# Tile slots, decay order and diagonal-block stores where DeltaNet periods meet mLSTM heads

## The chip, the cores and the metric

The kernel runs on one core of one Trainium2 chip. The metric is the device time of one execution in microseconds (us). The engines are TensorE (PE; its weight loads are a track of their own, PEld), VectorE (DVE), ScalarE (ACT), GpSimd (POOL) and SyncE (SP), which here issues the DMAs. Each engine takes its instructions in the order in which the program issued them.

## The reference

One decoder layer in float32, sequence 256, width 2048:

```
h = RMSNorm_pre(x) * (1 + scale) + shift        [shift | scale | gate] = silu(c) W_ada + b_ada
[gdn_qkv | a | b | gdn_z | ml_qk | ml_v | i | f | ml_o | ml_z | g_A | g_B] = h W_in
y_A = W_pA( RMSNorm_head(GatedDeltaNet(conv(q, k, v), decay, beta)) * silu(gdn_z) )
y_B = W_pB( sigmoid(ml_o) * RMSNorm_head(mLSTM(conv(q, k), v, i, f)) * silu(ml_z) )
out = (sigmoid(g_A) * y_A + sigmoid(g_B) * y_B) W_out
x <- x + gate * RMSNorm_post(out)
```

The DeltaNet branch has 16 query/key heads and 32 value heads of width 128, the mLSTM branch 8 heads with keys of 128 and values of 256. DeltaNet needs a triangular solve for each head; mLSTM needs decayed scores, their product with the values, and a normalisation.

## The kernel before

**A stream of weights.** All matmuls with weights go through one stream. A unit is a tile of 128 x 2048 weights (1 MB), loaded by SP into one of three buffers `raw` (L164). A unit has two pieces of 1024 columns; each is prepared by a cast on ACT (`whi`, L169) and a subtraction on DVE (`wlo`, L170), in four buffers each, up to four pieces ahead of PE. A product is then three matmuls, high by high, high by low and low by high (L223). A unit's load is issued once the unit three before it has been prepared.

**Side work in steps.** Everything else is written as generators. After each piece that PE uses, one side step runs every generator up to its next `yield`, in order of rank: the second half of a DeltaNet period first (rank 0), then scores, convolutions and mLSTM (rank 1), then the triangular solve (rank 2). So one program order, fixed when the kernel is built, says what stands behind what on each engine; `yield from wait(n)` puts work n steps later. A debt of DVE time holds the solve back (`side.room`); other generators wait for free PSUM banks (`banks`).

**The order of the stream.** After a start phase come eight DeltaNet periods. Each has the projection of an even head pair (8 pieces), a gate projection z (8) and the projection of an odd pair (8). Then come four pairs of mLSTM heads, m = 0 to 3: the q/k projection (tiles 24 + m), the v projection (28 + m), and for m = 0 also two gate projections (32 and 36). Then the projections `py` out of both branches and the output projection `pw`.

**A DeltaNet pair.** `gdn_stage1` does the convolution and Silu (L585 to L590), loads two rows of cumulated decays into `gb` (L603), masks them on POOL into `dd` (L610; one buffer), takes the score products on PE (`psa`, `psb`) and exponentiates `dd` on ACT (L618 to L620). DVE multiplies scores and decays into `au` (L677), the first block one step before the second. After the second pair of a period `base_inverse` stores the 32 x 32 diagonal blocks of both pairs' `au` into DRAM, four stores for each pair (`ud`, L697), loads them back spread over the partitions (`ug`, L701, four loads of 128 KB), and solves on DVE (L708 to L725; one buffer `ug`). The inverse goes out and back once more (`xd`, `xcmp`) and `gdn_stage2` carries on 31 steps later, or at once for the last period: small matmuls `mp`, `mx`, `mq`, `mz`, `pa`, `pb`, `pc`, `po` with ACT's copies between them (`pcm`, `y`, `ys`) and DVE's `rr` (L822); at the end the turned heads go through `oT` (two buffers) to `o_dr` (L884).

**An mLSTM pair.** `mlstm_qk` loads its own `gb`, does the convolution, and in the convolution's second and fourth step issues the mask (into the same `dd`) and the exps. When seven periods have passed `po`, it issues the scores `pss`, their product with the decays (`mst`, L931), then `pnum` against the values `vt` (copied out of PSUM by ACT, L993), squares, denominators, and `hn`. DVE multiplies `hn` by the gates (L1004, L1007); `mlstm_out` turns it on PE (`mpt`, L976), scales it on ACT into `hT` (L980), and stores it to `hb_dr`. `hT` uses the buffers of `oT`.

**The gate of the residual.** silu(c) times the last third of W_ada is summed by DVE: 16 more units of 1 MB in the same stream, in the same three buffers, with two DVE operations each (L1062, L1064, `gacc`) and no PE work. `add_gate_unit` is called once a tile and lets a unit in whenever 24 chunks have come up, 16 for each call; the calls are in the projections of m = 1, 2 and 3. At the end `gate_sum` adds the partitions on PE, and ACT copies the four quarters through one buffer `gr` (tag `ys`), each stored by SP before the next copy may write.

Of the kernel before, what the change touches and what calls it, by code (L numbers as in the profile page):

```python
# [7 lines left out]
F32 = mybir.dt.float32  # L8
# [109 lines left out]
def hybrid_layer_kernel(  # L118
# [99 lines left out]
    def pow_(o, i, e):  # L218
        G.tensor_tensor(o, i, e, op=ALU.pow)  # L219
# [402 lines left out]
    def gdn_stage1(p, ps, res):  # L622

        z = p % 2
        qs = bp.tile([P, 4, S], F32, name="qs", tag="qs")
        qh = bp.tile([P, 2, S], F32R, name="qh", tag="qh", bufs=1)
        yield from conv_silu(ps, lambda n, j: late_c["gcv"][:, (p * 4 + n) * 4 + j:(p * 4 + n) * 4 + j + 1], qs, qh,
                             0 if z else 3)
        gb = decay_rows(2 * p)
        dd = decay_mask(gb)  # L630
        b12 = bp.tile([P, 2], F32, name="b12", tag="b12")
        G.tensor_tensor(b12, gb[:, :, P - 1], ngt[:, 0, 2 * p:2 * p + 2], op=ALU.add)
        side.debt += 0.7
        ql = bp.tile([P, 2, S], F32R, name="ql", tag="ql", bufs=1)
        V.tensor_tensor(ql, qs[:, 0:2], qh.bitcast(F32), op=ALU.subtract)
        yield from wait(2)
        yield from banks(3)
        res["t"] = side.t
        psa = gtile("psa", True)
        mm3(psa, qh[:, 1, 0:P], ql[:, 1, 0:P], qh, ql, True, True)  # L640
        psb = gtile("psb", True)
        mm3(psb[:, 0:256], qh[:, 1, P:S], ql[:, 1, P:S], qh[:, :, P:S], ql[:, :, P:S], True, True)
        for m in range(2):
            T.transpose(psb[:, 256 + m * P:256 + (m + 1) * P], qs[:, 0, m * P:(m + 1) * P], ident)
        psv = gtile("psv", True)
        side.debt -= 1.6
        for blk in range(2):
            for h in range(2):
                T.transpose(psv[:, (blk * 2 + h) * P:(blk * 2 + h + 1) * P],
                            qs[:, 2 + h, blk * P:(blk + 1) * P], ident)  # L650
        decay_exp(dd, gb, ngt[:, 0, 2 * p:2 * p + 2], b12, ngt[:, 1, 2 * p:2 * p + 2])
        sse = bp.tile([P, 4], F32, name="sse", tag="sse", bufs=3)
        junk = bp.tile([P, P], F32, name="junk", tag="sq", bufs=1)
        for m in range(2):
            A.activation(junk, psb[:, 256 + m * P:256 + (m + 1) * P], AF.Square, accum_out=sse[:, m:m + 1])
        yield
        if z == 0:
            res["eq"] = bp.tile([P, 2, 2], F32, name="eq", tag="eq", bufs=3)
            res["rr"] = bp.tile([P, 2, 2, S], F32, name="rr", tag="rr")
        rk = bp.tile([P, 2], F32, name="rk", tag="rk")  # L660
        cj = bp.tile([P, 2, 2], F32, name="cj", tag="cj")
        res["au", z] = au = bp.tile([P, 2, 768], F32, name="au", tag="au", bufs=5)

        side.debt += 1.3
        for blk, ps_, n, c0 in ((0, psa, 256, 0), (1, psb, 128, 512)):
            V.scalar_tensor_tensor(au[:, 0, c0:c0 + P], ps_[:, n:n + P], 1.0, ident, op0=ALU.mult, op1=ALU.mult,
                                   accum_out=sse[:, 2 + blk:3 + blk])
        V.tensor_scalar(sse[:, 2:4], sse[:, 2:4], EPS, None, op0=ALU.add)
        V.reciprocal(rk, sse[:, 2:4])
        V.tensor_tensor(cj, tt[:, :, 32 + 2 * p:34 + 2 * p], rk.unsqueeze(2).broadcast_to([P, 2, 2]), op=ALU.mult)  # L670
        V.tensor_scalar(res["eq"][:, z], sse[:, 0:2], EPS, 128.0 * EPS, op0=ALU.add, op1=ALU.mult)

        for blk, ps_, n, c0 in ((0, psa, 256, 0), (1, psb, 128, 512)):
            yield
            side.debt += 1.45 if blk == 0 else 1.0
            for h in range(2):
                V.scalar_tensor_tensor(au[:, h, c0:c0 + 2 * n].rearrange("p (a b) -> p a b", a=2),  # L677
                                       ps_[:, 0:2 * n].rearrange("p (a b) -> p a b", a=2), cj[:, blk, h:h + 1],
                                       dd[:, h, c0 // 2:c0 // 2 + n].unsqueeze(1).broadcast_to([P, 2, n]),
                                       op0=ALU.mult, op1=ALU.mult)  # L680
            gfree(ps_)
            if blk == 0:
                sk = bp.tile([P, 2], F32, name="sk", tag="sk")
                pow_(sk, sse[:, 2:4], phalf[:, 0:2])
        yield
        for blk in range(2):
            A.activation(res["rr"][:, blk, z], psv[:, blk * S:(blk + 1) * S], AF.Copy, scale=sk[:, blk:blk + 1])
        gfree(psv)

    def base_inverse(zg, res, zr):  # L690

        ud = dr.tile([4, 8, 32, 32], F32, name="ud", tag="ud", bufs=2)
        xd = dr.tile([8, 4, 4, 8, 32], F32, name="xd", tag="xd", bufs=2)
        for zi in range(2):
            auv = res["au", zi].rearrange("p h (b c) -> p (h b) c", b=2)
            for q in range(4):
                SP.dma_start(ud[q, 4 * zi:4 * zi + 4].rearrange("m j i -> j m i"),  # L697
                             auv[32 * q:32 * q + 32, :, 256 + 32 * q:288 + 32 * q])
        ug = bp.tile([P, 32, 32], F32, name="ug", tag="ug", bufs=1)
        for q in range(4):  # L700
            SP.dma_start(ug[32 * q:32 * q + 32],  # L701
# [207 lines left out]
    def mlstm_qk(m, ps, r):  # L909
# [2 lines left out]
        av = [tt[:, b, 64 + 2 * m:66 + 2 * m] for b in range(2)]  # L912
        conv = conv_silu(ps, lambda n, j: late_c["mcv"][:, (m * 4 + n) * 4 + j:(m * 4 + n) * 4 + j + 1], qk)
        for i, _ in enumerate(conv):
            if i == 1:
                ee = decay_mask(gb)
            elif i == 3:
                decay_exp(ee, gb, av[0], av[0], av[1])
            yield
        yield  # L920
        while applied[0] < 7:
            yield
# [45 lines left out]
    def mlstm_out(m, r):  # L968
        while "hn" not in r:
            yield  # L970
        hn = r["hn"]
        for h in range(2):
            pt = gtile("mpt")
            for cc in range(2):
                for b in range(2):
                    T.transpose(pt[:, cc * S + b * P:cc * S + (b + 1) * P], hn[h][:, b, cc * P:(cc + 1) * P], ident)  # L976
            hT = bp.tile([P, 2, S], F32, name="hT", tag="oT")
            for cc in range(2):
                ch = (2 * m + h) * 2 + cc
                A.activation(hT[:, cc], pt[:, cc * S:(cc + 1) * S], AF.Copy, scale=late_c["mnw"][:, ch:ch + 1])  # L980
            ch = (2 * m + h) * 2
            SP.dma_start(hb_dr[ch:ch + 2].rearrange("c d t -> d c t"), hT)
            yield

    def mlstm(m):
# [39 lines left out]
        def gated():  # L1025

            sg = bp.tile([P, 2, 512], F32, name="sg", tag="sz", bufs=3)
            SP.dma_start(sg, gate_dr[7 + m])
            yield from wait(2)
            while "hn" not in r:  # L1030
                yield
            yield
            for b in range(2):
                gate(b, sg[:, b], True)
            yield
            yield from mlstm_out(m, r)
        gate_unit = add_gate_unit if m else None
        add_proj_t(24 + m, lambda ps: side.add(mlstm_qk(m, ps, r)), gate_unit)
# [1 line left out]
        if m:  # L1040
            return
        add_proj_n(32 + m, lambda ps: gate_after(ps, AF.Sigmoid))
        add_proj_n(36 + m, lambda ps: gate_after(ps, AF.Silu))

    gate_at = [0, 0]
    gate_half = []
# [1 line left out]
    def add_gate_unit():  # L1048

        gate_at[1] += KC  # L1050
        if gate_at[1] < 24 or gate_at[0] == KC:
            return
        gate_at[1] -= 24
        i = gate_at[0]
        gate_at[0] += 1

        def prep(h, raw):
            side.debt += 2.4
            for q in range(2):
                if i == 0:  # L1060
                    gate_half.append(bp.tile([P, 1024], F32, name=f"gacc{q}", tag="au", bufs=5))
                    V.tensor_scalar(gate_half[q], raw[:, q * 1024:(q + 1) * 1024], sil[:, 0:1], None, op0=ALU.mult)  # L1062
                else:
                    V.scalar_tensor_tensor(gate_half[q], raw[:, q * 1024:(q + 1) * 1024], sil[:, i:i + 1],  # L1064
                                           gate_half[q], op0=ALU.mult, op1=ALU.add)
            if i == KC - 1:
                side.add(gate_sum())
            return ()
        stream.add(w_ada[32 + i], prep, None, 1)

    def gate_sum():
        yield
        for q in range(4):
            gps = gtile("gps")
            T.matmul(gps[0:1, :], ones, gate_half[q // 2][:, (q % 2) * 512:(q % 2 + 1) * 512], start=True, stop=True)
            gr = bp.tile([1, 512], F32, name="gr", tag="ys", bufs=1)
            A.copy(gr, gps[0:1, :])
            yield
            SP.dma_start(gate_row_dr[:, q * 512:(q + 1) * 512], gr)
# [288 lines left out]
```

## Time and profile before

| | |
|---|---|
| median of 3 runs | 1625.53 us (1624.24 to 1626.09) |
| the profiled execution | 1628.82 us |
| its span, first to last instruction | 1627.0 us |
| mean granted TensorE clock | 0.998 |
| DMA | 372.37 MB, mean 229 GB/s |

The span is cut by stage as follows: up to about 330 us the start, 330 to 1000 the DeltaNet periods, 1000 to 1300 the passage into and through the mLSTM heads, 1300 to 1600 the projections out, then the tail. In the rows of the profile, `L170` is line 170 of the kernel, `out<-in` are the program's names of what an instruction writes and reads, and "idle before" tells how long the engine stood still and which instruction or DMA ended that. Matmuls overlap, so a matmul's duration is longer than its spacing to the next.

### The profile page before, as it was taken

The numbers are of one execution on the slowest core, as the hardware profiler recorded it, in microseconds if no ns is written. First come the engines' busy times: TensorE is split into PE (matmuls) and PEld (weight loads), VectorE is DVE, ScalarE is ACT, GpSimd is POOL, SyncE is SP. The second block draws the span as 40 slices with busy tenths as digits, with TensorE's granted clock in tenths as the row PEclk, the third lists the DMA queues.
The fourth block names the chain that finished last, engine by engine and source line by source line (L and its number), as shares of the span: only waits on it lengthen the run. The fifth ranks groups of instructions, "written<-read, shape, count | busy, mean of one in ns | idle before, by whom it ended". The sixth has DMA issues, their size and how long they took to land. (4 is left out here: it accounts for less than half of the span.)

```text
span 1627.0 us, 25444 instructions
## 1 busy us (share of the span) xinstructions
PE 1590.7 (98%) x9844; PEld 1388.0 (85%) x9844; DVE 1148.0 (71%) x1798; ACT 932.5 (57%) x1496; POOL 234.2 (14%) x191
## 2 busy tenths in 40 slices
PE   7999999899999999999999999999999999999998
PEld 4788888689999999999999999789887788888886
DVE  6685555665689787878787878685778556756654
ACT  7754446665656575757575756565565544444442
POOL 1787761000000000000000100000000000100100
PEclk9999999999999999999999999999999999999999
DMA  9898775665465545555555455547788668766573
GB/s 378 334 408 329 267 285 183 242 253 196 163 202 173 186 165 185 179 181 180 180 181 180 168 177 190 160 164 263 266 313 316 223 236 300 275 238 246 200 272 117
DMA packets 96261, 372.37 MB, mean 229 GB/s; under 512 B 26262, under 2 KB 46214, under 8 KB 58252
## 3 DMA queue, kind: packets, MB, share of 16 engines
q1 hardware_dynamic: 96140, 370.75, 64.3%
q8 instruction: 77, 1.26, 0.3%
q14 instruction: 44, 0.36, 0.1%
HBM read 354.40 MB, written 16.31 MB: 228 GB/s over the span
## 5 line engine op out<-in xcount | busy, mean ns | idle before, releaser
L170 DVE TENSOR_TENSOR wlo<-raw,whi 128x1024 fp32r<-128x1024 f32 x454 | 561.0, 1245 | 253.4 <-ACT whi L169 252.3
L169 ACT CAST whi<-raw 128x1024 fp32r<-128x1024 f32 (+1 forms) x517 | 530.3, 1046 | 304.8 <-PE pn L223 136.7
L223 PE MATMUL pt<-h_hi,whi 128*128 128x256 f32 x1280 | 368.8, 288 | 0.0
L223 PE MATMUL pt<-h_hi,wlo 128*128 128x256 f32 x1280 | 363.0, 284 | 0.0
L223 PE MATMUL pt<-h_lo,whi 128*128 128x256 f32 x1280 | 362.8, 283 | 0.0
L223 PE MATMUL pn<-whi,h_hi 128*128 128x512 f32 x896 | 354.3, 395 | 8.2 <-ACT whi L169 6.2
L223 PE MATMUL pn<-wlo,h_hi 128*128 128x512 f32 x896 | 352.3, 393 | 6.1 <-DVE wlo L170 5.2
L223 PE MATMUL pn<-whi,h_lo 128*128 128x512 f32 x896 | 350.2, 391 | 0.0
L223 PEld LDWEIGHTS pt<-h_hi,whi 128*128 128x128 f32 x1280 | 245.9, 192 | 1.4
L223 PEld LDWEIGHTS pt<-h_lo,whi 128*128 128x128 f32 x1280 | 245.9, 192 | 0.3
L223 PEld LDWEIGHTS pt<-h_hi,wlo 128*128 128x128 f32 x1280 | 245.8, 192 | 0.2 <-DVE wlo L170 0.2
L223 PEld LDWEIGHTS pn<-wlo,h_hi 128*128 128x128 f32 x896 | 168.9, 188 | 47.4 <-DVE wlo L170 13.1
L223 PEld LDWEIGHTS pn<-whi,h_hi 128*128 128x128 f32 x896 | 168.9, 188 | 46.6 <-ACT whi L169 7.0
L223 PEld LDWEIGHTS pn<-whi,h_lo 128*128 128x128 f32 x896 | 168.8, 188 | 34.8
L170 POOL TENSOR_TENSOR wlo<-raw,whi 128x1024 fp32r<-128x1024 f32 (+1 forms) x63 | 146.3, 2332 | 67.0 <-ACT whi L169 64.2
L223 PE MATMUL py<-whi,yhi 128*128 128x512 f32 x384 | 150.7, 392 | 1.2 <-ACT vt L993 1.2
L223 PE MATMUL py<-whi,ylo 128*128 128x512 f32 x384 | 149.6, 389 | 0.0
L223 PE MATMUL py<-wlo,yhi 128*128 128x512 f32 x384 | 149.4, 389 | 0.0
L409 DVE TENSOR_TENSOR part<-pn,part 128x512 f32<-128x512 f32 x112 | 73.5, 684 | 52.7 <-PE pn L223 52.7
L169 ACT CAST yhi<-ya 128x512 fp32r<-128x512 f32 x48 | 29.8, 622 | 128.4 <-PE py L223 124.2
L170 DVE TENSOR_TENSOR ylo<-ya,yhi 128x512 fp32r<-128x512 f32 x48 | 33.2, 692 | 90.5 <-ACT yhi L169 88.6
L585 DVE SCALAR_TENSOR_TENSOR qs<-pt,gcv,qs 128x255 f32<-128x255 f32 (+2 forms) x192 | 92.1, 480 | 4.6
(244 smaller groups left out, 1782.2 us busy)
## 6 DMA issues: line engine op xcount, KB each, us to landing
raw<-in_dram SPq DMA_DIRECT2D x259, 1024.0 KB
ar<-in_dram SPq DMA_DIRECT2D x32, 1024.0 KB
raw<-in_dram SPq DMA_DIRECT2D x16, 512.0 KB
ya<-o_dr SPq DMA_DIRECT2D x32, 256.0 KB
gate_dr<-part SPq DMA_DIRECT2D x11, 512.0 KB
gb<-rows SPq DMA_DIRECT2D x20, 256.0 KB
raw<-in_dram SPq DMA_DIRECT2D x6, 768.0 KB
ug<-ud SPq DMA_DIRECT2D x32, 128.0 KB
```

Source lines behind the costliest of these rows:

```text
L169: A.copy(hi, src)
L170: (eng or V).tensor_tensor(lo, src, hi.bitcast(F32), op=ALU.subtract)
L223: T.matmul(ps, l, r, start=start and i == 0, stop=stop and i == 2, skip_group_check=True)
L409: V.tensor_tensor(part[g][:, b], ps[b], part[g][:, b], op=ALU.add)
L585: V.scalar_tensor_tensor(dst[:, n, sh:], src[:, 0:S - sh], taps(n, 3 - sh), dst[:, n, sh:], op0=ALU.mult, op1=ALU.add)
```

## The change

- The stores of the diagonal blocks (`ud`) move out of `base_inverse` into `block_rows`, called for each pair in the step of its last score product.
- A counter `scored` tells which pair that was. `mlstm_qk` goes on past the convolution only when it is 15; for m = 0 the mask is then issued one step later and the exps two steps later, no longer within the convolution. For m = 1 to 3 they stay in the convolution.
- `hT` takes the buffers `qh` and `ql` in turn.
- After the gates of m = 1 to 3, `mlstm_out` starts two steps later where it was one.
- Gate units are let in also during the second gate projection of m = 0 (4 more calls, 28 in all), one for every 28 chunks; there are still 16, and the last comes with the same call.
- The two sums `gacc` take a buffer of `ug` and one of `rr` where they had two of the five of `au`; the four quarters `gr` take buffers of `on` (two), `p2` and `tmp`.

```diff
@@ gdn_stage1
             if blk == 0:
                 sk = bp.tile([P, 2], F32, name="sk", tag="sk")
                 pow_(sk, sse[:, 2:4], phalf[:, 0:2])
+            else:
+                scored[0] = p
+        block_rows(res, z)
         yield
...
+    scored = [-1]
+
+    def block_rows(res, z):
+
+        if z == 0:
+            res["ud"] = dr.tile([4, 8, 32, 32], F32, name="ud", tag="ud", bufs=2)
+        auv = res["au", z].rearrange("p h (b c) -> p (h b) c", b=2)
+        for q in range(4):
+            SP.dma_start(res["ud"][q, 4 * z:4 * z + 4].rearrange("m j i -> j m i"),
+                         auv[32 * q:32 * q + 32, :, 256 + 32 * q:288 + 32 * q])
+
     def base_inverse(zg, res, zr):
-        ud = dr.tile([4, 8, 32, 32], F32, name="ud", tag="ud", bufs=2)
+        ud = res["ud"]
         xd = dr.tile([8, 4, 4, 8, 32], F32, name="xd", tag="xd", bufs=2)
-        for zi in range(2):
-            auv = res["au", zi].rearrange("p h (b c) -> p (h b) c", b=2)
-            for q in range(4):
-                SP.dma_start(ud[q, 4 * zi:4 * zi + 4].rearrange("m j i -> j m i"),
-                             auv[32 * q:32 * q + 32, :, 256 + 32 * q:288 + 32 * q])
@@ mlstm_qk
         for i, _ in enumerate(conv):
-            if i == 1:
+            if i == 1 and m:
                 ee = decay_mask(gb)
-            elif i == 3:
+            elif i == 3 and m:
                 decay_exp(ee, gb, av[0], av[0], av[1])
             yield
+        while scored[0] < 2 * 7 + 1:
+            yield
+        if m == 0:
+            yield
+            ee = decay_mask(gb)
+            yield
+            decay_exp(ee, gb, av[0], av[0], av[1])
         yield
@@ mlstm_out
-            hT = bp.tile([P, 2, S], F32, name="hT", tag="oT")
+            hT = bp.tile([P, 2, S], F32, name="hT", tag=("qh", "ql")[h], bufs=1)
@@ mlstm, gated
-            yield
+            yield from wait(2)
             yield from mlstm_out(m, r)
...
-        add_proj_n(36 + m, lambda ps: gate_after(ps, AF.Silu))
+        add_proj_n(36 + m, lambda ps: gate_after(ps, AF.Silu), add_gate_unit)
@@ add_gate_unit
-        if gate_at[1] < 24 or gate_at[0] == KC:
+        if gate_at[1] < 28 or gate_at[0] == KC:
             return
-        gate_at[1] -= 24
+        gate_at[1] -= 28
...
-                    gate_half.append(bp.tile([P, 1024], F32, name=f"gacc{q}", tag="au", bufs=5))
+                    gate_half.append(bp.tile([P, 1024], F32, name=f"gacc{q}", tag=("ug", "rr")[q], bufs=1 + q))
@@ gate_sum
-            gr = bp.tile([1, 512], F32, name="gr", tag="ys", bufs=1)
+            gr = bp.tile([1, 512], F32, name="gr", tag=("on", "on", "p2", "tmp")[q], bufs=(2, 2, 1, 1)[q])
```

## The prediction

> **What bounds the kernel now.** I read the page first, then the busy time of the engines by stage, then TensorE's (PE's) waits in the one stage that has any, then the rows behind each.
>
> ```profile
> span 1627.0 us, 25444 instructions
> ```
>
> ```profile
> 330.00:1000.00 670.00, 669.18 (x5261) 625.93 (x5261) 531.11 (x1032) 423.28 (x732) 37.91 (x68) 1.00 0.55 184
> 1000.00:1300.00 300.00, 289.77 (x1808) 247.88 (x1807) 211.44 (x324) 173.11 (x326) 18.35 (x22) 0.99 0.69 241
> 1300.00:1600.00 300.00, 299.38 (x1337) 247.68 (x1336) 182.51 (x185) 139.52 (x170) 14.57 (x8) 1.00 0.70 251
> ```
>
> Each row has the stretch, its length, then busy us and instructions of PE, PE's weight loads, DVE, ACT and POOL, the granted clock, the DMA share and GB/s. PE is the bound. In the DeltaNet periods (330 to 1000 us) it idles 0.8 us of 670; only 1000 to 1300, where the periods give way to the mLSTM heads, is open: 10.2 us idle, and a clock a little under full. The start lies outside the change. From the last row, with nothing but 512-column products, one takes 300 / 1336 = 0.22 us, a piece of twelve 2.7. So the ceiling is near 12 us, 0.7%. The waits of that stage (total us, times, longest):
>
> ```profile
> PE pn L223 <- DVE wlo L170: 2.7, 3, 1.1
> PE pnum L947 <- issue: 1.3, 1, 1.3
> PE mq L790 <- ACT y L780: 1.3, 1, 1.3
> PE pn L223 <- ACT whi L169: 1.2, 1, 1.2
> PE py L223 <- ACT vt L993: 1.2, 1, 1.2
> PE mpt L976 <- DVE hn L1004: 1.0, 2, 0.6
> PE pc L829 <- DVE rr L822: 0.9, 1, 0.9
> PE psa L223 <- DVE ql L635: 0.5, 1, 0.5
> ```
>
> Eleven stops, 10.1 us: the whole idle time. The question is which the change reaches. I count the side steps from step 0, in which pair 15's scores go to PE; its last score product is issued in step 3.
>
> **Part 1: decays of head pair 0 behind the last scores.** Rows of the timeline, here and below: start, busy us, engine, line, operation, tiles; in brackets the idle time before and what ended it.
>
> ```profile
> 1021.28 0.77 POOL L610 TENSOR_SCALAR_AFFINE_SELECT dd<-gb 128x256 f32<-128x256 f32 x2 [14.45 <-DVE au L677]
> 1021.72 0.40 ACT L618 ACTIVATE dd<-dd,tt 128x128 f32<-128x128 f32 x1 [8.34 <-POOL dd L610]
> ...
> 1023.49 1.03 ACT L169 CAST whi<-raw 128x1024 fp32r<-128x1024 f32 x1
> 1022.96 0.39 PE L223 MATMUL pn<-whi,h_lo 128*128 128x512 f32 x1
> 1024.57 0.50 PE L223 MATMUL pn<-whi,h_hi 128*128 128x512 f32 x1 [1.23 <-ACT whi L169]
> 1025.83 0.50 PE L223 MATMUL pn<-wlo,h_hi 128*128 128x512 f32 x1 [0.76 <-DVE wlo L170]
> ```
>
> The head's mask takes the only dd buffer, so POOL waits for the last reader of pair 15's (L677); ACT, in order, sits on the exps 8.34 us with the weight casts (whi) behind them, until PE runs dry: 1.2 us, and a wlo wait of 0.8 us next. Now the mask is issued in step 7 and the exps in step 8, when dd has long been free. Both stops go. From 1022.96 to 1024.57 is 1.61 us, of which 1.23 idle and 0.22 the usual spacing: a stop costs some 0.15 beyond its idle time.
>
> What is added: Silu of this head (step 5) now precedes the exps, so one more table load.
>
> ```profile
> 1005.00 1.28 ACT L618 ACT_TABLE_LOAD   x1
> 1006.30 0.40 ACT L618 ACTIVATE dd<-dd,ngt 128x128 f32<-128x128 f32 x1
> ...
> 1032.46 1.06 ACT L993 COPY vt<-pn 128x512 f32<-128x512 f32 x2
> 1033.54 0.76 ACT L768 COPY pcm<-mp 32x256 f32<-32x256 f32 x2
> ...
> 1035.61 0.38 ACT L780 ACTIVATE y<-mx 32x256 f32<-32x256 f32 x1 [0.24 <-PE mx L778]
> ```
>
> Load 1.28 and exps 1.77 (1021.72 to 1023.49) make 3.1 us of ACT in step 8, behind which stand one whi and y, which mq reads in step 10. From the end of step 8's matmuls ACT needs about 2.0 (vt, pcm), 3.1, 1.0 and 0.4: y at 6.5; PE gets to mq after two pieces of 2.7 and two groups of small matmuls, at about 6.5. I take 0.1, between nothing and the whole 3.1. The scores that read the exps are issued only in step 17, so nothing else waits.
>
> By the Trainium skill, "ScalarE: Activation LUTs", section "What ACT_TABLE_LOAD costs", a switch also drains for some 1.38 us, 2.66 in all, which would hold mq 1.3 longer and give 1616.3 instead of 1615.0. The trace disagrees: the first exp starts 1.30 us after the load does.
>
> **Part 2: diagonal blocks out pair by pair.**
>
> ```profile
> 1020.29 8.40 SPq L164 DMA_DIRECT2D raw<-in_dram  x2
> 1028.75 0.94 SPq L884 DMA_DIRECT2D o_dr<-oT  x2
> 1029.73 6.04 SPq L697 DMA_DIRECT2D ud<-au  x8
> 1036.37 2.76 SPq L701 DMA_DIRECT2D ug<-ud  x4
> 1039.18 0.92 SPq L164 DMA_DIRECT2D raw<-in_dram  x2
> 1046.49 0.17 DVE L708 TENSOR_SCALAR nsu<-ug 128x15 f32<-128x15 f32 x1 [7.39 <-DMA ug<-ud]
> 1050.00:1075.00 25.00, 22.12 (x116) 18.02 (x115) 24.06 (x46) 14.10 (x30) 0.00 (x0) 1.00 0.40 136
> ```
>
> The eight ud stores and four ug loads stand together in SP's queue and hold it about 9 us: ug lands at 1046.5, after DVE has idled 7.39 us, and the next raw loads are issued only at 1039.18. DVE then runs 24.06 of 25 us to catch up, and PE meets it late three times: twice on wlo (the 2.7 us above less part 1's 0.8, so 1.9) and once on rr (0.9). Now pair 14's four stores left 24 steps before, and pair 15's four follow its last score product: SP takes them at about 1021, between the raw load at 1020.29 and the next, which waits for a later wlo anyway. Before the loads of ug only o_dr remains; without part 1's stall ug is issued near 1028 and, at the old 7 to 10 us from issue to use, is there at 1035 to 1038, when DVE gets there (PE is 2.3 us earlier, so about 1037). Raw loads follow 4 to 9 us sooner. I count all three stops as gone, with nothing gone as the other end. What is queued behind a store's wait is SP's next raw load; in the 330 to 1000 stage the same twelve DMAs stood ahead of raw loads in every period and PE idled 0.8 us, so I cost the earlier places there at nothing.
>
> **Part 3: own place for hT.**
>
> ```profile
> 1103.59 0.84 ACT L980 ACTIVATE hT<-mpt,mnw 128x256 f32<-128x256 f32 x2 [5.55 <-DMA o_dr<-oT]
> 1107.10:1110.50 3.40, 3.40 (x18) 3.40 (x18) 2.14 (x2) 1.82 (x3) 0.00 (x0) 0.51 0.86 315
> ```
>
> hT shares two buffers with oT, whose stores must land first: ACT idles 5.55 us, y comes late, mq waits 1.3. In qh and ql, last read in step 0, it waits for nothing. Right after that stop the granted clock is 0.51 for 3.4 us, 3.4 x 0.49 = 1.7 us lost; I take it as a result of the stop and the small matmuls around it, so it goes too.
>
> **Part 4: the gate's units, sums and row; one more step for mpt.**
>
> ```profile
> 1146.68 2.47 DVE L1064 SCALAR_TENSOR_TENSOR gacc<-raw,sil,gacc 128x1024 f32<-128x1024 f32 x2
> 1155.44 1.04 ACT L169 CAST whi<-raw 128x1024 fp32r<-128x1024 f32 x1 [6.82 <-DMA raw<-in_dram]
> ...
> 1270.83 0.58 ACT L1077 COPY gr<-gps 1x512 f32<-1x512 f32 x1 [5.14 <-DMA gate_row_dr<-gr]
> 1093.99 1.43 DVE L1007 TENSOR_TENSOR hn<-hn,sg 128x256 f32<-128x256 f32 x4
> 1096.94 0.66 PE L976 MATMUL mpt<-con,hn 128*128 128x128 f32 x4
> ```
>
> Raw has three buffers. At 1155 the load that ACT awaits reuses a gate unit's, so it could be issued only after that unit's 2.47 us on DVE ended at 1149.15; vt stands behind that cast, pnum behind vt: the stop called "issue". With 16 units over 28 places the second tile of head pair 2's projection (t26) reuses the last v tile's buffer instead, one to three pieces sooner; I count 1.3 as gone (other end: none). The old pattern now stands at head pair 2's end, where no DeltaNet work is beside it: I take 0.0, at most 1.5.
>
> gr with a place for each quarter drops the wait of 5.14 us in ACT ahead of head pair 3's squares; its hn is gated that much sooner, and mpt comes a step later: both stops (1.0) go. The later step delays only stores into hb_dr that are read long after.
>
> Two units now start beside the last gate projection. The first comes after the triangle solve in DVE's queue; the second puts 2.47 us ahead of L1007. That ended at 1095.4, so now about 1097.9, past mpt's 1096.94; mpt needs three quarters of it first. I take a new stop of 0.8 (0 to 2.5).
>
> **Sum.** Gone: 2.7 + 1.3 + 1.3 + 1.2 + 1.0 + 0.9 = 8.4 of idle time, nine stops x 0.15 = 1.35, the clock's 1.7: 11.4. Stay: py (1.2; nothing of the change stands ahead of that vt copy in ACT's queue) and psa. New: 0.9. Net 10.5. The profiled execution took 1628.8 around its span of 1627.0, so 1618.3; the median shown, 1625.5, is 3.3 lower, and gives 1615.0.
>
> **Rivals.**
> - *DVE's load, not ug, makes it late* (24.06 of 25 speaks for it; 330 to 1000, with the same solve and no stops, against): 1.9 + 0.9 idle and three fills of 0.15 stay, 3.3 more: 1618.3, and to 1622 if pnum's stop and a larger mpt stop stay too.
> - *The clock dip isn't the stop's.* The idle time before it is only 1.3 us. If it comes by itself it stays: 1.7 more, 1616.7. The Trainium skill, "TensorE: Matmul & The Clock Gate", section "Why this matters for your kernels", sides with this: it asks only for no idle gap over some 3 us. By that rule 1616.7; the dip's own row and the absence of another in 1000 to 1300 don't settle it.
> - *The waits move.* The edits work, but raw loads or DVE stop PE elsewhere for as much: 1622.3 to 1628.8, no change.
> - *Slower: SP.* Pair by pair, the even pairs' four stores now sit in SP's queue behind their last score product, ahead of weight loads, in all eight periods. Four take 3.0 us (6.04 / 2). If raw had no slack that is up to 8 x 3.0 = 24: 1639. Above 1.3 a period (10.5 / 8) it ends slower than before. Against it: PE's 0.8 us idle in 330 to 1000 under a 9 us hold of the same queue.
>
> **Chances.** Forecast 0.55 (1612.7 to 1618), DVE's load 0.17, clock 0.09, waits move 0.12, SP 0.07. A measurement of this kernel can tell about 0.2% (3.3 us) from no change; faster by more: 0.55 + 0.17 + 0.09 = 0.81. The range holds these three: low end with py's stop gone too and no new ones (11.4 + 1.35 = 12.8 off), high end where the first rival ends.
>
> **What would show it.** Right: in 1000 to 1300 idle PE of 2 to 3 us instead of 10.2; no ACT wait for POOL dd, o_dr or gate_row_dr there; DVE's wait for ug under 2 us; an Exp table load after the head's Silu; a clock of 1.00 up to the tail. Wrong: wlo stops that stay near 1050 to 1060 (first rival), a 0.5 clock again (second), whi waiting for raw with PE stopped behind it in the gate stretch (third) or before 1000 (fourth).

## The result and the profile after

| | before | changed |
|---|---|---|
| median device time | 1626.05 us (1623.5 to 1631.1, 7 runs) | 1617.33 us (1613.7 to 1621.1, 7 runs) |
| ratio to before | | 0.9943 (95% interval 0.9926 to 0.9960) |
| span of the profiled execution | 1627.0 us | 1615.0 us |
| PE idle in the passage, 1000 to 1300 (changed: to 1290) | 10.2 us | 3.2 us |

The change makes the kernel 0.57% faster, 8.7 us on the medians; the forecast was 10.5 us. The busy time by stage, changed kernel, columns as before:

```profile
330.00:1000.00 670.00, 669.82 (x5281) 628.08 (x5280) 534.26 (x1037) 428.69 (x739) 38.84 (x68) 1.00 0.55 186
1000.00:1290.00 290.00, 286.81 (x1796) 247.84 (x1795) 210.11 (x321) 173.17 (x321) 18.72 (x22) 0.99 0.70 247
```

and PE's waits in the second of these stretches, in total, times, longest:

```profile
PE mpt L992 <- DVE hn L1023: 1.8, 2, 1.5
PE pt L888 <- DVE on L879: 0.7, 1, 0.7
PE pnum L963 <- issue: 0.6, 1, 0.6
```

The eleven stops of before are gone. Four stand in their place, at hn and at the transposes ahead of it (2.5 us together) and at pnum of head pair 2 (0.6).

Where the profiled 12 us came from is read from one instruction that both kernels have: the first score product of DeltaNet pair 0 and of pair 15 (psa), and the first product of the merge (mtp). Timeline of PE, before:

```profile
401.93 0.40 PE L223 MATMUL psa<-qh 128*128 128x512 f32 x1
...
1003.49 0.40 PE L223 MATMUL psa<-qh 128*128 128x512 f32 x1
...
1405.08 0.27 PE L1174 MATMUL mtp<-con,mg 128*128 128x128 f32 x1
```

and changed:

```profile
401.67 0.40 PE L223 MATMUL psa<-qh 128*128 128x512 f32 x1
...
1000.98 0.40 PE L223 MATMUL psa<-qh 128*128 128x512 f32 x1
...
1393.10 0.27 PE L1190 MATMUL mtp<-con,mg 128*128 128x128 f32 x1
```

From psa of pair 0 to that of pair 15 it was 601.6 us and is 599.3: 2.3 us came out of the periods, where I had seen nothing to gain. From there to the merge it was 401.6 us and is 392.1: 9.5 us out of the passage.

Two of the main reasons, in the changed kernel's rows. First the decays: the table load and the exps now stand where they hold up nobody, and y follows at 1031.1.

```profile
1026.96 1.28 ACT L618 ACT_TABLE_LOAD   x1
1028.26 0.40 ACT L618 ACTIVATE dd<-dd,tt 128x128 f32<-128x128 f32 x1
...
1031.09 0.37 ACT L789 ACTIVATE y<-mx 32x256 f32<-32x256 f32 x1
```

No wait on POOL's dd is left before step 8, and PE has no stop at mq there. Second the diagonal blocks: SP's queue, DVE, and the busy times of the stretch in which DVE solves.

```profile
1015.91 0.33 SPq L164 DMA_DIRECT2D raw<-in_dram  x1
1016.70 1.75 SPq L701 DMA_DIRECT2D ud<-au  x4
1021.81 0.35 SPq L164 DMA_DIRECT2D raw<-in_dram  x1
1022.26 0.90 SPq L893 DMA_DIRECT2D o_dr<-oT  x2
1023.25 2.93 SPq L710 DMA_DIRECT2D ug<-ud  x4
```

```profile
1036.42 0.17 DVE L717 TENSOR_SCALAR nsu<-ug 128x15 f32<-128x15 f32 x1 [1.85 <-DMA ug<-ud]
```

```profile
1038.00:1063.00 25.00, 25.00 (x138) 21.64 (x137) 23.80 (x50) 14.39 (x31) 0.00 (x0) 1.00 0.38 135
```

Four stores instead of eight stand ahead of ug, DVE's wait falls from 7.39 to 1.85 us, and PE is busy all 25 us while DVE is as full as before (23.80 against 24.06). One thing did not go: a stretch at half clock, now behind the stop at hn.

```profile
1092.20:1095.60 3.40, 3.40 (x17) 3.21 (x16) 3.40 (x4) 0.95 (x2) 0.00 (x0) 0.50 0.70 186
```

### The profile page after: what moved, and what is told of

Read it like the earlier page. It is cut to its first block, busy times and chain, and to the rows that moved or that the text cites. A ratio compares the mean times of both kernels' runs of the same rounds, so it can differ in the third digit from the quotient of the medians.

```text
span 1615.0 us, 25449 instructions
## 1 busy us (share of the span) xinstructions
PE 1585.7 (98%) x9844; PEld 1388.1 (86%) x9844; DVE 1148.3 (71%) x1798; ACT 936.4 (58%) x1497; POOL 235.2 (15%) x191
## 4 chain that ended last, share of the span: by engine, by line
PE 88%; DVE 3%; ACT 3%; issue 2%; DMA 2%; POOL 1%; SPq 0%; DVEq 0%; POOLq 0%; ACTq 0%
PE pn L223 31%; PE pt L223 29%; PE py L223 16%; PE pw L223 5%; ACT whi L169 2%; DVE wlo L170 1%; DMA raw<-in_dram 1%; DVE part L409 1%; PE psa L223 1%; DMA ar<-in_dram 1%; PE mz L808 1%; PE mq L799 1%; PE po L848 0%; PE pa L820 0%; PE pc L838 0%
```

## The experiments

### One part at a time

Each of these is the kernel before with one of the four parts of the prediction; the edits are those of the diff above. They share their runs of the kernel before (median 1627.55 us).

**Part 1 alone.**

> The kernel before with part 1 alone (decays of head pair 0 behind the last scores). Theory (each stop of PE belongs to the edit that was held against it): the stops on whi and wlo near 1023 to 1026 us go (2.0 us idle, two fills of 0.15), ACT's wait of 8.3 us for POOL's dd goes; DVE still waits some 6 to 7 us for ug, so the three stops behind it (2.8 us) stay, and mq's stop and the 0.5 clock after it stay. Time 1626.05 - 2.3 = 1623.8. Rival (DVE's load of 24 of 25 us is what stops PE at 1050 to 1063): same here, the three stops stay. Rival (waits only move): the time stays within 1 us of 1626.

Measured: 1626.14 us, ratio 0.9987 (0.9974 to 1.0000). The stops near 1023 to 1026 went, as the theory had it. Of the three behind ug, two stayed (1.0 us on wlo, 1.0 on rr). But its profiled execution, the slowest of its twelve, had longer stops at pnum and three stretches at half clock; its largest wait of the passage is

```profile
PE pnum L958 <- issue: 4.4, 2, 2.6
```

in place of 1.3. How long pnum waits differs from one execution to the next: in two profiles of the changed kernel it was 0.6 and 0.9 us. The part is worth about its 2 us, at the edge of what can be measured.

**Part 2 alone.**

> The kernel before with part 2 alone (diagonal blocks out pair by pair). Theory: whi and wlo near 1023 to 1026 stay; DVE's wait for ug in the last period falls from 7.4 to under 2 us, and the three stops at 1050 to 1063 (2.8 us idle) go: 1626.05 - 3.3 = 1622.8. Rival (DVE's load): the wait for ug goes as well, but the three stops stay, and the time is within 1 us of 1626. Rival (SP): raw loads behind the even pairs' stores come late and PE idles more than 0.8 us in 330 to 1000.

Measured: 1622.26 us, ratio 0.9959 (0.9947 to 0.9971), 6.7 us, the largest of the four. DVE and PE's waits:

```profile
1040.15 0.17 DVE L713 TENSOR_SCALAR nsu<-ug 128x15 f32<-128x15 f32 x1 [4.43 <-DMA ug<-ud]
```

```profile
PE pc L834 <- DVE rr L827: 0.8, 1, 0.8
PE pn L223 <- DVE wlo L170: 0.8, 1, 0.8
```

DVE's wait fell only to 4.4 us: part 1's stall is still ahead of it, and the loads of ug are issued at 1026.4 here, at 1023.3 in the changed kernel. Yet both wlo stops behind it went (the 0.8 left is the one near 1021) and only rr's stayed. Against the expectation the whi stop near 1024 went too; ACT's exps start at 1018.4 here, in place of 1021.7. The rival of DVE's load falls with this row and with the full DVE of the changed kernel: the same solve stops nobody when its start isn't late. The SP rival falls too: from psa of pair 0 to pair 15 this kernel takes 599.7 us against 601.6, so the early stores cost the periods nothing. Of the kernels profiled here, the five without part 2 took 600.4 to 602.6 us for this stretch, the changed kernel, part 2 alone and the last version without stops below 599.3 to 599.7. So the stretch is even shorter with part 2, by 0.7 us or more, with one execution profiled for each kernel.

**Part 3 alone.**

> The kernel before with part 3 alone (hT in the buffers of qh and ql). Theory: ACT's wait of 5.6 us for o_dr and PE's stop at mq (1.3 us) go, and with them the 0.5 clock at 1107: 1.45 + 1.7 = 3.1 us, 1622.9. Rival (the clock's dip comes by itself): the stop goes, a stretch of 3.4 us at 0.5 stays somewhere in 1000 to 1300: 1624.6.

Measured: 1623.72 us, ratio 0.9975 (0.9963 to 0.9987), 4.1 us. The passage, columns as above:

```profile
1000.00:1300.00 300.00, 292.29 (x1826) 250.54 (x1825) 213.88 (x327) 175.20 (x328) 17.40 (x22) 1.00 0.71 246
```

The stop at mq is gone, and the theory's 3.1 lies in the interval (2.1 to 6.0), the rival's 1.4 does not. In this execution the clock is 1.00 throughout the passage. That is not so in every one: the mean clock of its six runs is 0.9980, from 0.996 to 0.999, against 0.9978 for the 24 runs of the kernel before. The time speaks for more than the stop's own 1.4 us; that the rest is the clock's is not shown.

**Part 4 alone.**

> The kernel before with part 4 alone (16 gate units over 28 places, sums and row in other buffers, mpt of pairs 1 to 3 one step later). Theory: the stops at pnum of pair 1 (1.3), at mpt of pair 3 (1.0) and, as in the changed kernel, at py (1.2) go, with four fills 4.1 us; a stop at mpt of pair 0 of 2 to 3 us is new, as in the changed kernel, where mpt and the transposes before it stood 2.5 us: net -1 to -2, 1624 to 1625. Rival (waits only move): the new stop takes back all of it, 1626.

Measured: 1629.56 us, ratio 1.0008 (0.9998 to 1.0018): no gain. The stops at pnum of pair 1 and at mpt of pair 3 went; one of 1.4 at pnum came at pair 2, and where the first early units stand came

```profile
PE mpt L976 <- DVE hn L1007: 1.5, 1, 1.5
```

with 1.0 at the transposes before it and 6.8 us at half clock behind them. The rival had this one right: the new stops take back everything. (The profiled execution, 1632.6 us, is one of the two slowest of its eleven.) The four parts alone add up to 2.1 + 6.7 + 4.1 - 1.3 = 11.6 us, the whole change gave 9.3 by its ratio; with intervals of 2 us on each that agrees.

### The new stop at hn

The prediction put it there, by the second early gate unit's 2.47 us on DVE ahead of hn. The changed kernel's SP queue at that place says something else:

```profile
1062.96 2.91 SPq L164 DMA_DIRECT2D raw<-in_dram  x2
1065.92 0.43 SPq L737 DMA_DIRECT2D xd<-xx  x1
1072.35 2.75 SPq L740 DMA_DIRECT2D xcmp<-xd  x4
1075.20 3.43 SPq L164 DMA_DIRECT2D raw<-in_dram  x3
```

```profile
1080.18 2.00 ACT L169 CAST whi<-raw 128x1024 fp32r<-128x1024 f32 x2 [6.43 <-PE pn L223]
```

```profile
1081.26 1.23 DVE L170 TENSOR_TENSOR wlo<-raw,whi 128x1024 fp32r<-128x1024 f32 x1 [2.98 <-ACT whi L169]
```

The two loads from 1063 on are weights and the second early unit's megabyte. (The recorded expectations call it the first unit's. But DVE reads the first unit from 1064.1 to 1065.5, and the second of the two loads is issued right behind that, into the buffer that this frees.) xd is stored behind them, and the loads of xcmp wait in SP until xd has landed: 6.0 us after its issue, against 4.1 in the kernel before. The weight loads behind xcmp go out only from 1075.2 on. ACT's cast waits 6.43 us until 1080.18. (The profile puts that wait down to pn, which had been done for long. The cast starts 5.0 us after the issue at 1075.2; that it waited for that load's landing is inferred.) DVE then idles 2.98 us. Two theories, then: SP's hold, or the second unit's work on DVE.

**xcmp two steps later**, with what follows where it was:

```diff
         SP.dma_start(xd.rearrange("qq q rg m i -> (q rg m) qq i"), xx)
         xcmp = bp.tile([P, 8, 32], F32, name="xcmp", tag="xcmp", bufs=1)
+        yield from wait(2)
         for q in range(4):
             SP.dma_start(xcmp[32 * q:32 * q + 32], xd[:, q])
-        yield from wait(5)
+        yield from wait(3)
```

> The changed kernel with the four loads of xcmp issued two side steps later after the store of xd (and the wait behind them two steps shorter, so that the solve's successor stands where it stood). In the changed kernel PE stops at 1085.9 to 1090.2 us on DVE (on, hn; 2.5 us idle) and a 0.5 clock follows. Theory SP: the loads of xcmp wait in SP's queue until xd has landed, which the first early gate unit's megabyte delays; weight loads behind them are issued at 1075.2 only, so ACT's cast waits 6.4 us until 1080.2 and DVE 3.0 us for it. Then here that wait of ACT falls under 2 us, the stops on on and hn fall under 0.7 us, the dip goes: 3 to 5 us less than 1617.3, 1612.5 to 1614.5. Theory DVE (the one the prediction used): the second early unit's 2.5 us ahead of hn makes it late. Then the stops stay at 2 us or more, 1616.5 to 1618.

Measured: 1613.81 us, ratio 0.9911 (0.9896 to 0.9926), beside runs of the kernel before with a median of 1629.10 us, which the next three share. SP's queue and PE's waits in the passage:

```profile
1066.54 0.43 SPq L737 DMA_DIRECT2D xd<-xx  x1
1068.43 0.33 SPq L164 DMA_DIRECT2D raw<-in_dram  x1
1073.14 2.75 SPq L741 DMA_DIRECT2D xcmp<-xd  x4
1075.99 0.39 SPq L164 DMA_DIRECT2D raw<-in_dram  x1
```

```profile
PE pnum L964 <- issue: 0.6, 1, 0.6
PE mpt L993 <- DVE hn L1024: 0.2, 1, 0.2
```

The weight load that waited until 1075.2 goes out at 1068.4. The unit's DVE work is all still there; the stops at hn fall from 2.5 us to 0.2, and the half clock is gone.

**The second unit's DVE work cut** to 8 of 1024 columns (its share of the gate sum is mostly left out):

```diff
+                elif i == 1:
+                    V.scalar_tensor_tensor(gate_half[q][:, 0:8], raw[:, q * 1024:q * 1024 + 8], sil[:, i:i + 1],
+                                           gate_half[q][:, 0:8], op0=ALU.mult, op1=ALU.add)
```

> The changed kernel, the second gate unit's two DVE operations cut to 8 of 1024 columns each (this leaves out most of that unit's share in the gate sum); its load stays. Theory DVE: 2.4 us of DVE less ahead of on and hn, so the stops at 1085.9 to 1090.2 fall from 2.5 us idle to under 0.5, and the dip goes: 1613 to 1614. Theory SP: DVE stood idle 3.0 us right behind that unit, waiting for ACT's cast, so nothing moves: stops within 0.5 us of 2.5, time 1616.5 to 1618.

Measured: 1618.96 us, ratio 0.9944 (0.9925 to 0.9963): level with the changed kernel, and a microsecond above what SP's theory gave. DVE:

```profile
1076.88 0.36 DVE L1080 SCALAR_TENSOR_TENSOR gacc<-raw,sil,gacc 128x8 f32<-128x8 f32 x2
1082.68 1.22 DVE L170 TENSOR_TENSOR wlo<-raw,whi 128x1024 fp32r<-128x1024 f32 x1 [5.44 <-ACT whi L169]
```

2.1 us less work became 2.5 us more waiting for the cast (5.44 for 2.98), and the stops stayed: 1.8 at mpt and 1.0 at the transposes. The prediction's reason for its own new stop is refuted, and by the run before this one SP's hold is shown. This run leaves the unit's load in place, so it doesn't separate the two ways in which the load can harm: ahead of xd in the queue, or by the one of three raw buffers that the unit keeps until DVE has read it.

**The units back over 24 places** in the changed kernel (the call in the projection 36 and the 28 undone):

> The changed kernel with the gate units back where they were (16 over the 24 places of head pairs 1 to 3; sums and row keep their new buffers). Both theories of the stop at mpt: no unit stands beside the last gate projection, so the stops on on and hn of 2.5 us idle and the dip behind them go. Theory of part 4 (a load that reuses a gate unit's buffer is late): the stop at pnum of pair 1 comes back, 1.3 us, and the one of 0.6 at pair 2 goes. Net 1.5 to 4 us less than the changed kernel: 1613 to 1616. Rival (spreading the units is what took part 4's stops away and more): slower than 1618.

Measured: 1615.95 us, ratio 0.9922 (0.9907 to 0.9936). No stop at hn; pnum of pair 1 stops again for 1.2, and two more came in the v projection of pair 2:

```profile
PE pnum L963 <- issue: 1.4, 2, 1.2
PE pn L223 <- DVE wlo L170: 0.8, 1, 0.8
PE pn L223 <- ACT whi L169: 0.7, 1, 0.7
```

The loads of xcmp wait 4.3 us for xd here, as in the kernel before. So spreading the units does take stops away; without the cure for xcmp it gives back at least as much.

**xcmp and mpt of pair 0 two steps later:**

```diff
             if not first:
+                yield from wait(2)
                 yield from mlstm_out(m, r)
```

> The changed kernel with xcmp's loads two steps later and head pair 0's mpt two steps later too. Theory SP: no stop over 0.7 us at on or hn; at most 1 us idle in 1000 to 1290 against 3.2: 1612 to 1614.5, the same as with xcmp alone or up to 1 us less. Theory DVE: mpt's stop (1.8 us) goes by the later place, the 0.7 on the transposes stays: 1614 to 1616.

Measured: 1613.43 us, ratio 0.9906 (0.9890 to 0.9922), level with xcmp alone. No stop at on or hn; in its profiled execution the one at pnum of pair 2 was 2.3 us, more than the 1 us expected for all.

**The same, and part 4 alone with xcmp later; the changed kernel again.** The last stop stands where vt's copy is behind a cast that waits for raw, 7.2 us in the profile above. A step more ahead of pnum:

```diff
         while "vt" not in r:
             yield
-        yield
+        yield from wait(2 if m else 1)
```

> The changed kernel with xcmp's loads two steps later, head pair 0's mpt two steps later and pnum of pairs 1 to 3 one step later. Theory (what is left are casts of vt that come behind one late weight load, so a step more hides them): no stop over 0.5 us in 330 to 1290 and no 0.5 clock there: 1611 to 1613, 0.990 of before or less, with little spread. Rival (the late load holds more than vt): a stop on whi or wlo takes the place of pnum's, and the time stays at the 1613.4 of the kernel without this step.

> The kernel before with part 4 and xcmp's loads two steps later. Part 4 alone was no faster than before (1629.6, ratio 1.0008). Theory SP: the early gate unit behind which xd lands late, with weight loads held behind xcmp, cost it its gain; here the stops on on and hn (2.5 us idle, 3.8 with their fills) go and the time is 3 to 5 us under part 4 alone, ratio 0.997 to 0.9985. Rival (part 4's gain is lost elsewhere): ratio 1.000 within its interval, the stops stay or others stand in their place. The wait for hT and its stop at mq are still in it.

> The changed kernel once more, beside the two below on one chip. Expected 0.9943 of before, as first measured, with its stops at on and hn near 1086 to 1090 us (2.5 us idle) and at pnum of pair 2 (0.6 or more).

Measured beside one set of runs of the kernel before (median 1627.25 us): the version with all three steps 1611.93 us, ratio 0.9899 (0.9885 to 0.9914), all runs within 1611.5 to 1613.5; part 4 with xcmp later 1623.98, 0.9979 (0.9966 to 0.9992); the changed kernel 1620.03, 0.9936 (0.9919 to 0.9953). PE in the passage of the first:

```profile
1000.00:1285.00 285.00, 285.00 (x1800) 246.80 (x1799) 210.87 (x321) 173.34 (x322) 16.08 (x22) 1.00 0.72 253
```

It has no idle time left there: this version beats both kernels, by 1.0% and by about 0.4%. Part 4, worth nothing alone, gains 0.2% together with xcmp's later loads: its stops at on and hn fell to 0.3 us, though its stop at mq (hT still in oT's place) grew to 2.9. What xcmp's step alone gives to the kernel before was not run, so the 0.2% isn't shared out between the two. The changed kernel's ratio repeats; the profiled execution of this repetition was one of its quickest (1612.8 us, the stops at mpt 0.7 us), while four of its six runs took 1620.0 to 1620.6. In that profile the loads of xcmp waited 5.1 us, in the first one 6.0: the hold lasts longer in some executions than in others. That it makes the slower runs is not shown, as these were not profiled.

### Does a stop bring the half clock?

In the thirteen profiles up to here, twelve stretches at half clock ("dips"; one of them double) lie between 330 and 1300 us, each beginning within 5 us of the start of a stop of PE of over 1.2 us. All in all there are 29 stops of over 1 us, so 17 have no dip behind them; the version without stops has none. To see it without the mLSTM heads, three copies of rr onto itself ahead of y in each period of that version:

```diff
+        rf = res["rr"].rearrange("p b z s -> p (b z s)")
+        for _ in range(3):
+            A.activation(rf, rf, AF.Copy, scale=1.0)
         A.activation(y0[32:64, :, 0:32], cols32(psx[0], S)[32:64], AF.Copy, scale=-1.0)
```

> The kernel without stops (f4_pnum_later) with three copies of rr onto itself (1.06 us each) ahead of ACT's y in each of the eight periods, so that PE stops about 1 to 2 us at mq eight times, six or seven of them in 330 to 1000 us, where no profile so far has a clock below 1.00. Theory (a stop of 1 to 3 us brings a 0.5 clock of 3.4 us in about one case of three or four, by where it falls): one to four dips of 3.4 us, each within 5 us behind one of these stops and none elsewhere. Rival (the dips come by themselves in the passage to the mLSTM heads): none in 330 to 1000.

Measured: 1619.22 us in one execution (the kernel before beside it: 1625.40). PE's waits from 330 to 1290, and a stretch behind the longest:

```profile
PE mq L803 <- ACT y L793: 4.8, 7, 2.0
```

```profile
1040.00:1043.40 3.40, 3.40 (x11) 2.60 (x10) 2.32 (x9) 2.46 (x3) 0.00 (x0) 0.50 0.51 210
```

The six stops in the periods came out too short for the test, 0.5 us each, and no dip followed one. The seventh, 2.0 us from 1037.0 on, was followed by the only dip before the tail. That speaks for the stop as the cause, but in the passage again; for the periods the question stays open.

The traces tell more about which stops bring a dip. The profile of part 1 alone has three:

```profile
1104.42:1107.83 3.41, 3.41 (x19) 3.41 (x18) 2.43 (x3) 1.88 (x4) 0.00 (x0) 0.50 0.94 315
1155.62:1159.03 3.41, 3.41 (x12) 2.90 (x12) 2.60 (x6) 2.69 (x11) 0.00 (x0) 0.50 0.99 411
1210.23:1213.64 3.41, 3.41 (x14) 3.09 (x14) 2.74 (x3) 2.75 (x10) 0.00 (x0) 0.50 0.95 333
```

They begin 51.20 and 54.61 us apart, 15 and 16 times the 3.413 us that each lasts, and in every profile here the changes of the clock lie whole multiples of 3.413 us apart: they fall on a grid. Sorted by the cells of that grid, all fourteen profiles, 330 to 1300 us: PE idle for more than 1.5 us in one cell was followed by a dip in 10 of 10 cases, for 1.2 to 1.5 us in 3 of 12, for less in none (the double dip counted once). The stop of 2.9 us in part 4 with xcmp later lies across a mark: 1.4 us in one cell, no dip, and 1.5 in the next, then the dip. No run shifted a stop against the grid, so this is a reading of the traces and not an experiment.

## Why the prediction was right, and where not

- **The bound and the ceiling** were right: PE, about 12 us, in the passage. It missed 2.3 us in the periods, where idle time was 0.7 us between the two score products and is nothing now. The other 1.5 us lie in the spacing of matmuls that the profile counts as busy. Part 2 accounts for some of it, as far as single executions tell.
- **The total.** 1615.0 was forecast and 1617.33 measured, near the upper end of the range, 1618. (The range's text also puts that end where the first rival ends, which is 1622 in the rival's own words; the measured time lies inside either way.) That the sum came so near is in part luck: part 2 alone gave 3.4 us more than its terms, part 4 alone some 3.3 less than its 1.3 + 1.0 + 0.45 - 0.8. Of the signs of being right, the idle time came out at 3.2 where 2 to 3 was named, and the clock was not 1.00 up to the tail. The waits that were to leave ACT (for POOL's dd, for o_dr ahead of hT, for gate_row_dr) did leave it.
- **Part 1** was right: both stops went, the second table load costs 1.28 us of ACT and nothing of PE. y is done at 1031.5 and nothing waits for it. The drain of 1.38 us that the Trainium skill states, in "ScalarE: Activation LUTs", section "What ACT_TABLE_LOAD costs", would have shown as a later exp. The first exp starts 1.30 us after the load does, as before, so the measurement decides against it.
- **Part 2** was right in mechanism (ug's wait, SP's queue) and too small in size: 3.3 us forecast, 6.7 measured alone (4.7 to 8.6). By the profiles the rest is in the periods (up to 1.9 us), and in the whi stop that went with it (1.2 and its fill).
- **Part 3** was right in the wait and near in size, 3.1 against 4.1 us. Its clock term of 1.7 us is borne out by the one profile of part 3 alone and not by the mean clock of all its runs; it stays open.
- **Part 4**: the stops that it was to remove went. The new stop was forecast at 0.8 us in the right place for a wrong reason, which is luck. It measured 2.5 us and brought a dip; what makes it is weight loads held behind xcmp, once the second early unit's load is there. The prediction followed the moved units through DVE's queue and not through SP's, where xcmp's wait stands. The 0.6 at pnum of pair 2 is the one that it named and took at nothing.
- **py's stop**, which it kept, went. No edit was meant for it, and no other profile here has one over 0.3 us; it belonged to that one execution.
- **The sum** for the passage was 10.5 us and measured 9.5: one dip more than forecast (1.7), a longer new stop (1.7) and pnum (0.6), less py (1.35) and what was left of psa (0.5). These give 8.4, so about 1.1 us of the gain in the passage isn't accounted for.
- **The rivals**: DVE's load, SP and "the waits move" fell as told above, the last except for hn. The clock rival was right in its sign, a 0.5 clock again, and its 1616.7 lies nearer to the measured time than 1615.0. But the dip stands elsewhere, behind a new stop, and not by itself. The Trainium skill, "TensorE: Matmul & The Clock Gate", section "Why this matters for your kernels", asks only for no idle gap over some 3 us. Here dips followed stops of 1.2 to 2.9 us, so the measurement decides against that rule at this length, while not every stop brings one.

## What to carry to other kernels

When work is moved to another place in a stream, follow it through every in-order queue that it enters, the DMA issuer's first of all: a load that waits for the landing of a store holds back all loads behind it in that queue, and here one more unit of a megabyte was enough to turn a harmless wait into a stop of PE, by way of ACT and DVE. Put a few steps between a store and the load that reads it back. In a kernel bound by PE, a stop of a microsecond or two is worth more than its idle time: here it cost some 0.15 us until the matmuls were dense again, and sometimes 1.7 us of clock.

## What was not expected of the hardware

The granted clock fell to half for about 3.4 us (6.8 once) behind stops of PE of only 1.2 to 2.9 us, twelve times for 29 stops of over 1 us, and this is likely a good part of the spread between executions: the changed kernel's seven runs lie between 1613.7 us at a mean clock of 0.999 and 1621.1 at 0.996, the version without stops between 1611.5 and 1613.5. The 0.003 of clock between those two is an estimated 4.9 us of their 7.4. The dips begin on a grid of 3.413 us, and the idle time within one cell of it tells most cases apart, not how long the whole stop is; for 1.2 to 1.5 us in a cell it stays open why some bring a dip and others do not.
